# One encoder layer with a mixture of experts: the block arena closes behind the router, and expert weights are loaded four rows of a partition at a time

## The chip, the core and the metric

The kernel runs on one core of a Trainium2 chip. The core has five engines with instruction streams of their own: PE (matrix products), DVE and ACT (elementwise work), POOL (GpSimd) and SP, which in this kernel only issues DMAs and reads registers. Sixteen DMA engines move data between the chip's HBM and the core's SBUF, a memory of 128 partitions. The metric is the device time of one execution in microseconds (us); less is better. Of the kernel before three runs were timed: median 1249.86 us, from 1247.67 to 1251.27.

## What is computed

One layer for 256 tokens of width 1024, all in float32. Cut to what matters here:

```python
mod = silu(c) @ w_ada + b_ada                      # six vectors: shift, scale, gate for each half
h = x * (1 + scale1) + shift1
q_a, k_a, v_a, c_q, c_kv, k_rope, g_a, g_b = split(h @ w_in)
y_a = chunked_relpos_attention(q_a, k_a, v_a);  y_b = mla_attention(c_q, c_kv, k_rope)
merged = sigmoid(g_a) * (y_a @ w_branch_a) + sigmoid(g_b) * (y_b @ w_branch_b)
x = layer_norm(ALPHA * x + gate1 * (merged @ w_out), ln1_g, ln1_b)
h = x * (1 + scale2) + shift2
logits = h @ w_router + b_router                   # top 4 of 32 experts, softmax over the 4
f = sum over the 4 experts of weight * ((up + 1) * g * sigmoid(1.702 * g)) @ w_down[e] + ...
    # g = min(h @ w_gate[e] + b_gate[e], 7), up = clip(h @ w_up[e] + b_up[e], -7, 7)
x = layer_norm(ALPHA * x + gate2 * f, ln2_g, ln2_b)
```

Each of the 32 experts has three matrices of 1024 x 1024 float32, 4 MB each: 384 MB of weights that are read once.

## The kernel before

SBUF holds an **arena** `ar` of twenty blocks of 128 x 2048 float32 (8 KB of a partition, 1 MB each). `al()` takes the block that has been free the longest, `fr()` gives blocks back; a new tile on a block waits until the old one's readers are done. All large things live in such blocks one after the other: the activations, weights of the dense part in pieces, and later the expert weights. Small things that live long are in the pool `keep`, those of the middle phase in `p3` on the right side, those of the experts in `mp`.

The order of the instructions on each engine isn't that of the code: a scheduler places them by its own estimate of when each can run. So an edit in one place can move instructions elsewhere.

The program has three stretches.

- *Projections and attention* (to about 190 us). Products that need full float32 precision are made from a high and a low part of each operand: `split` (L150 to L153) casts the high part on ACT and subtracts it, L153, on DVE or POOL (each takes half of a block), and `mm3` multiplies high by high, high by low and low by high (L279 to L281). Meanwhile `w_ada` streams in and DVE sums it up (L640).
- *The middle* (about 190 to 293 us). The modulation vectors are finished (L687 to L752): POOL copies rows to all partitions with `partition_broadcast` (L739, L740, L745). `load_branch` brings `w_branch_a` and `w_branch_b` in four pieces (L765), splits each (DVE the half of branch a, POOL that of branch b), and PE makes `ba` and `bb` from them; `load_wo` does the same for `w_out` (L808) and PE makes `o`. Then come the first norm, the router and the gathering of tokens (`route`, `gather_first`, `weigh`).
- *The experts* (from 293 us). The tokens of an expert are gathered with a 0/1 matrix. First comes the group `s`, the experts 30 and 31; the other 30, sorted by load, fall into 13 groups of two or three, `e0` to `e12`, whose numbers SP reads from `order_i` at run time (L1285, 30 register loads). For each group and each of the three kinds (gate, up, down) `load_group` issues the weights on SP and 8 k-steps of matmuls use them (L1063: `sg`, `su`, `sd`, `e0g` and so on).

In `load_group` a partition's eight rows of 1024 floats are brought in four loads of two rows, 1 MB each:

```python
for kq in range(4):
    for j in range(n):
        v, r = al()
        v = v.rearrange("p (k n) -> p k n", k=2)
        if not (fine and kq == 3):
            SP.dma_start(v, aps[j][:, 2 * kq:2 * kq + 2, :])
```

and `mm` frees a block after every second k-step. For the last kind of the last group (`fine`) the last two rows come in two halves of the columns. Ahead of the middle's branch loads `hold(4)` (L756) takes four blocks out of the arena, which are given back behind the router (`freed.update(held)`). SP can issue expert weights into these four long before the experts begin. `take_late` takes two blocks for the experts' activations, `load_norm` two for the final norm. The hooks of the group `s` sort the experts: `sort_a` (counts and ranks, L1147 to L1157), `sort_b` (`order_i`, L1161, L1162), `sort_c` (`tokp`, L1172).

## Time and profile before

| | |
|---|---|
| median of 3 runs | 1249.86 us (1247.67 to 1251.27) |
| the profiled execution | 1245.99 us, span 1244.3 us |
| PE busy | 1103.0 us, 89% of the span |
| DVE, ACT, POOL busy | 362.8, 172.5, 123.0 us (29%, 14%, 10%) |
| read from HBM | 459.09 MB, 370 GB/s over the span |
| chain that ended last | DMA 48%, PE 36%, DVE 8%, issue 3% |

The span is the time between the first and the last instruction that the profiler recorded; the execution's own time is 1.7 us more. A busy share is an average over stretches that are limited by different things. The profile's idle times name the engine or the DMA that released an instruction; "issue" means that nothing was recorded that it waited for. DMA shares are shares of all 16 engines.

### The profile page before, as it was taken

How to read it: one execution, taken by the hardware profiler on the slowest of the kernel's cores; microseconds unless marked ns; L12 is line 12 of the kernel's file. 1: busy time of each engine (PE TensorE's matmuls, PEld its weight loads, DVE VectorE, ACT ScalarE, POOL GpSimd, SP SyncE). 2: the span in 40 equal slices, each digit the busy share in tenths (PEclk: the TensorE clock that was granted, in tenths of full speed). 3: DMA queues.
4: the chain of work that ended last, by engine and by line, in shares of the span. 5: the costliest groups of instructions: out<-in, count | busy, mean ns of one | idle time of the engine just before them, and what ended most of it. 6: DMA issues, size and time to landing. Idle time of an engine off the chain costs nothing.

```text
span 1244.3 us, 19465 instructions
## 1 busy us (share of the span) xinstructions
PE 1103.0 (89%) x8023; PEld 511.9 (41%) x8023; DVE 362.8 (29%) x704; ACT 172.5 (14%) x340; POOL 123.0 (10%) x140
## 2 busy tenths in 40 slices
PE   6889999797998989899989789889889999899995
PEld 4658885773242433434223223232233434343431
DVE  4868982684121121211012001011011211111113
ACT  3345552230000000000000000000000000000011
POOL 2211562433000000000000000000000000000001
PEclk8989998898999999899999999999999999999998
DMA  9958646398999999999999999999999999999992
GB/s 341 345 186 307 229 142 237 102 355 333 421 420 420 421 422 420 422 420 420 421 421 421 421 420 421 422 421 420 422 421 421 421 420 421 420 420 421 421 399 76
DMA packets 90333, 461.44 MB, mean 371 GB/s; under 512 B 8809, under 2 KB 33430, under 8 KB 39298
## 3 DMA queue, kind: packets, MB, share of 16 engines
q1 hardware_dynamic: 90242, 460.17, 91.6%
q8 instruction: 64, 1.05, 0.3%
q14 instruction: 27, 0.22, 0.0%
HBM read 459.09 MB, written 1.05 MB: 370 GB/s over the span
## 4 chain that ended last, share of the span: by engine, by line
DMA 48%; PE 36%; DVE 8%; issue 3%; SPq 2%; ACT 1%; POOL 1%; DVEq 0%; ACTq 0%; POOLq 0%
DMA blk<-in_w_down_dram 19%; DMA blk<-in_w_up_dram 14%; DMA blk<-in_w_gate_dram 13%; DVE blk L640 1%; PE e2d L1063 1%; PE e0d L1063 1%; PE sg L1063 1%; PE e12d L1063 1%; PE e3d L1063 1%; PE e1d L1063 1%; PE sd L1063 1%; PE e3u L1063 1%; PE e2u L1063 1%; PE e1u L1063 1%; PE e0u L1063 1%
## 5 line engine op out<-in xcount | busy, mean ns | idle before, releaser
L153 POOL TENSOR_TENSOR blk<-blk,blk 128x512 fp32r<-128x512 f32 (+2 forms) x44 | 84.8, 1948 | 148.8 <-ACT blk L152 80.5
L1298 POOL COPY sel<-sel 96x64 bf16<-96x64 bf16 (+2 forms) x30 | 5.9, 230 | 807.5 <-PE e5d L1132 90.4
L152 ACT CAST blk<-blk 128x512 fp32r<-128x512 f32 (+2 forms) x76 | 54.1, 767 | 41.5 <-DVE blk L798 16.6
L1092 ACT ACTIVATE blk<-blk 128x512 f32<-128x512 f32 x28 | 17.2, 630 | 234.0 <-DVE blk L1090 234.0
L153 DVE TENSOR_TENSOR blk<-blk,blk 128x512 fp32r<-128x512 f32 (+2 forms) x32 | 39.0, 1227 | 33.7 <-ACT blk L152 23.0
L640 DVE SCALAR_TENSOR_TENSOR blk<-blk,csil,blk 128x1024 f32<-128x1024 f32 x28 | 41.8, 1537 | 1.3 <-DMA blk<-in_w_ada_dram 1.2
L281 PE MATMUL g<-blk,blk 128*128 128x256 f32 x128 | 36.6, 291 | 2.0 <-POOL blk L153 2.0
L279 PE MATMUL g<-blk,blk 128*128 128x256 f32 x128 | 36.8, 288 | 0.0
L280 PE MATMUL g<-blk,blk 128*128 128x256 f32 x128 | 36.1, 282 | 0.0
L1063 PE MATMUL e7u<-blk,xgb 128*32 128x512 f32 x128 | 25.3, 599 | 4.5 <-DMA blk<-in_w_up_dram 4.5
L1063 PE MATMUL e5u<-blk,xgb 128*32 128x512 f32 x128 | 25.6, 599 | 4.0 <-DMA blk<-in_w_up_dram 4.0
L1063 PE MATMUL e6u<-blk,blk 128*32 128x512 f32 x128 | 25.3, 599 | 4.0 <-DMA blk<-in_w_up_dram 4.0
L1063 PE MATMUL e5d<-blk,xgb 128*32 128x512 f32 x128 | 23.2, 656 | 3.6 <-DMA blk<-in_w_down_dram 3.4
L281 PEld LDWEIGHTS g<-blk,blk 128*128 128x128 f32 x128 | 24.2, 191 | 4.3 <-POOL blk L153 2.9
L1063 PE MATMUL e7d<-blk,blk 128*32 128x512 f32 x128 | 22.7, 597 | 3.0 <-DMA blk<-in_w_down_dram 2.7
L279 PEld LDWEIGHTS g<-blk,blk 128*128 128x128 f32 x128 | 24.5, 191 | 0.9 <-issue 0.6
L1063 PE MATMUL e6d<-blk,xgb 128*32 128x512 f32 x128 | 22.4, 621 | 2.5 <-DMA blk<-in_w_down_dram 2.5
L1063 PE MATMUL e4d<-blk,blk 128*32 128x512 f32 x128 | 22.1, 613 | 2.8 <-DMA blk<-in_w_down_dram 2.8
L280 PEld LDWEIGHTS g<-blk,blk 128*128 128x128 f32 x128 | 24.5, 191 | 0.0
L1063 PE MATMUL e4u<-blk,xgb 128*32 128x512 f32 x128 | 20.6, 596 | 2.0 <-DMA blk<-in_w_up_dram 2.0
L1063 PE MATMUL e6g<-blk,blk 128*32 128x512 f32 x128 | 19.4, 596 | 1.8 <-DMA blk<-in_w_gate_dram 1.8
L1063 PE MATMUL e7g<-blk,xgb 128*32 128x512 f32 x128 | 19.4, 595 | 1.7 <-DMA blk<-in_w_gate_dram 1.7
(745 smaller groups left out, 1919.2 us busy)
## 6 DMA issues: line engine op xcount, KB each, us to landing
blk<-in_w_gate_dram SPq DMA_DIRECT2D x128, 1024.0 KB, 19.7
blk<-in_w_up_dram SPq DMA_DIRECT2D x128, 1024.0 KB, 19.8
blk<-in_w_down_dram SPq DMA_DIRECT2D x126, 1024.0 KB, 19.8
blk<-in_w_ada_dram SPq DMA_DIRECT2D x24, 1024.0 KB, 9.6
blk<-in_w_in_dram SPq DMA_DIRECT2D x12, 1024.0 KB, 5.4
blk<-in_w_in_dram SPq DMA_DIRECT2D x8, 592.0 KB, 11.4
blk<-in_w_out_dram SPq DMA_DIRECT2D x4, 1024.0 KB, 6.0
blk<-in_w_branch_a_dram SPq DMA_DIRECT2D x4, 512.0 KB, 3.7
```

Of the source, the lines that this page charges most:

```text
L152: A.copy(hi, src)
L153: (V if eng == "V" else G).tensor_sub(lo, src, hi.bitcast(F32))
L279: T.matmul(o, sh, mh, start=first, stop=False)
L280: T.matmul(o, sh, ml, start=False, stop=False)
L281: T.matmul(o, sl, mh, start=False, stop=last)
L640: eng.scalar_tensor_tensor(acc_v[:, sl], v[:, q * D:(q + 1) * D], csil[:, k:k + 1], acc_v[:, sl], op0=ALU.mult, op1=ALU.add)
L1063: T.matmul(pss[hf][c0:c0 + m, :], stat[:, k, c0:c0 + m], ch[par][k // 2][:, k % 2, hf * 512:(hf + 1) * 512], start=(k == 0), stop=(fine an ...
L1092: A.activation(s, g[:, sl], AF.Sigmoid, scale=SW_ALPHA)
L1298: G.tensor_copy(sel[:, lo:lo + n], sel96[:, r:r + 1].to_broadcast([96, n]))
```

## The change

- The arena is no longer open to the end. Behind the router it is closed, and a new pool `ax` takes its bytes with ten blocks `wt0` to `wt9` of 128 x 4096 (16 KB of a partition, 2 MB). They are taken in the order in which pairs of the old blocks came free, by `al2` and `fr2`.
- `load_group` loads four rows of a partition in one DMA of 2 MB, in place of two of 1 MB; a block is freed after every fourth k-step. In the last kind the last four rows come as one load of two rows and two halves of the last two. `take_late` and `load_norm` take one big block each, and the loop for overfull experts (not run with these inputs) loads in the same way.
- `hold(4)` becomes `hold(0)`: no blocks are kept out of the arena, and so no expert weights can be issued before its blocks come free at the end of the middle.
- `keep` moves to the right side, below `p3`, and `mp` takes the bytes of `p3` on the right.

```diff
--- before.py
+++ after.py
@@ -117,7 +117,8 @@
 
     nb = [2]
     psum_phase("psum1")
-    ar = ctx.enter_context(tc.tile_pool(name="ar", bufs=1, side="left", reuse_waits="tile"))
+    ar_cm = tc.tile_pool(name="ar", bufs=1, side="left", reuse_waits="tile")
+    ar = ar_cm.__enter__()
     freed = {i: i - NB for i in range(NB)}
     clock = [0]
 
@@ -128,13 +129,15 @@
         clock[0] += 1
         return ar.tile([P, BLK], dt, tag=f"blk{i}", bufs=1, name=f"blk{i}_{clock[0]}"), i
 
-    held = {}
+    held = []
 
     def hold(n):
 
         for _ in range(n):
-            i = min(freed, key=freed.get)
-            held[i] = freed.pop(i)
+            i = min((i for i in range(0, NB, 2) if i in freed and i + 1 in freed),
+                    key=lambda i: max(freed[i], freed[i + 1]))
+            del freed[i], freed[i + 1]
+            held.append(i // 2)
 
     def fr(*blocks):
         for i in blocks:
@@ -670,9 +673,9 @@
     fr(hTh_r, hTl_r, qk_r, bva[0][1], bva[1][1])
 
     p2_cm.__exit__(None, None, None)
+    keep = ctx.enter_context(tc.tile_pool(name="keep", bufs=1, side="right", reuse_waits="tile"))
     p3_cm = tc.tile_pool(name="p3", bufs=1, side="right", reuse_waits="tile")
     p3 = p3_cm.__enter__()
-    keep = ctx.enter_context(tc.tile_pool(name="keep", bufs=1, side="left"))
 
 
     psum_phase("psum3")
@@ -753,7 +756,7 @@
     g2n, b2p = scale2, shift2
 
 
-    hold(4)
+    hold(0)
     for b in range(2):
         A.activation(gT[b], gT[b], AF.Sigmoid)
     WB = []
@@ -981,10 +984,30 @@
     fr(mgh_r, mgl_r, rt_r, ms_r, rwa_r, rwb_r)
 
     p3_cm.__exit__(None, None, None)
-
-
-    freed.update(held)
-    mp = ctx.enter_context(tc.tile_pool(name="mp", bufs=1, side="left", reuse_waits="tile"))
+    order_freed = sorted(range(NB // 2), key=lambda d: (d not in held, max(freed.get(2 * d, 0), freed.get(2 * d + 1, 0))))
+    ar_cm.__exit__(None, None, None)
+
+
+    ax = ctx.enter_context(tc.tile_pool(name="ax", bufs=1, side="left", reuse_waits="tile"))
+    mp = ctx.enter_context(tc.tile_pool(name="mp", bufs=1, side="right", reuse_waits="tile"))
+    slots_ax = [ax.tile([P, 2 * BLK], F32, tag=f"wt{d}", bufs=1, name=f"wt{d}_0") for d in range(NB // 2)]
+    fresh = set(range(NB // 2))
+    freed = {d: n for n, d in enumerate(order_freed)}
+    clock[0] = NB
+
+    def al2():
+        d = min(freed, key=freed.get)
+        del freed[d]
+        clock[0] += 1
+        if d in fresh:
+            fresh.discard(d)
+            return slots_ax[d], d
+        return ax.tile([P, 2 * BLK], F32, tag=f"wt{d}", bufs=1, name=f"wt{d}_{clock[0]}"), d
+
+    def fr2(d):
+        clock[0] += 1
+        assert d not in freed
+        freed[d] = clock[0]
 
 
     late = {}
@@ -993,7 +1016,8 @@
 
     def take_late():
         if not late:
-            a, b = al()[0], al()[0]
+            ab = al2()[0]
+            a, b = ab[:, 0:BLK], ab[:, BLK:2 * BLK]
             late["g"] = a[:, 0:D]
             late["s"] = [a[:, D + i * 512:D + (i + 1) * 512] for i in range(2)]
             late["y"] = [b[:, i * 512:(i + 1) * 512] for i in range(2)]
@@ -1006,19 +1030,21 @@
     def load_group(aps, fine=False):
         n = len(aps)
         ch, regs = [[] for _ in range(n)], [[] for _ in range(n)]
-        for kq in range(4):
+        for kh in range(2):
             for j in range(n):
-                v, r = al()
-                v = v.rearrange("p (k n) -> p k n", k=2)
-                if not (fine and kq == 3):
-                    SP.dma_start(v, aps[j][:, 2 * kq:2 * kq + 2, :])
+                v, r = al2()
+                v = v.rearrange("p (k n) -> p k n", k=4)
+                if not (fine and kh == 1):
+                    SP.dma_start(v, aps[j][:, 4 * kh:4 * kh + 4, :])
+                else:
+                    SP.dma_start(v[:, 0:2, :], aps[j][:, 4:6, :])
                 ch[j].append(v)
                 regs[j].append(r)
         if fine:
             for hf in range(2):
                 sl = slice(hf * 512, (hf + 1) * 512)
                 for j in range(n):
-                    SP.dma_start(ch[j][3][:, :, sl], aps[j][:, 6:8, sl])
+                    SP.dma_start(ch[j][1][:, 2:4, sl], aps[j][:, 6:8, sl])
         return ch, regs
 
     ptb = [pt0, mp.tile([P, 2, P], F32, name="pt1")]
@@ -1061,7 +1087,7 @@
             def step(k, hf):
                 for c0, m, par in segs:
                     T.matmul(pss[hf][c0:c0 + m, :], stat[:, k, c0:c0 + m],
-                             ch[par][k // 2][:, k % 2, hf * 512:(hf + 1) * 512],
+                             ch[par][k // 4][:, k % 4, hf * 512:(hf + 1) * 512],
                              start=(k == 0), stop=(fine and k == 7), skip_group_check=True)
 
             for k in range(8):
@@ -1073,9 +1099,9 @@
                 elif not (fine and k == 7):
                     for hf in range(2):
                         step(k, hf)
-                if k % 2 == 1:
+                if k % 4 == 3:
                     for rg in regs:
-                        fr(rg[k // 2])
+                        fr2(rg[k // 4])
                 if (name, k) in hooks:
                     hooks[(name, k)]()
             if not fine:
@@ -1233,7 +1259,8 @@
     fin = []
 
     def load_norm():
-        fin_v, o_v = al()[0], al()[0]
+        fo = al2()[0]
+        fin_v, o_v = fo[:, 0:BLK], fo[:, BLK:2 * BLK]
         lnr = o_v[0:1, :].rearrange("p (a n) -> p a n", a=2)
         SP.dma_start(lnr[:, 0, :], ln2_g)
         SP.dma_start(lnr[:, 1, :], ln2_b)
@@ -1322,10 +1349,10 @@
         def get_w(kind):
             ch, regs = [], []
             src = dyn_rows(weights[kind], e_dyn)
-            for kq in range(4):
-                v, r = al()
-                v = v.rearrange("p (k n) -> p k n", k=2)
-                SP.dma_start(v, src[:, 2 * kq:2 * kq + 2, :])
+            for kh in range(2):
+                v, r = al2()
+                v = v.rearrange("p (k n) -> p k n", k=4)
+                SP.dma_start(v, src[:, 4 * kh:4 * kh + 4, :])
                 ch.append(v)
                 regs.append(r)
             return [ch], [regs]
```

Up to the router the lines of the changed kernel are those of before plus 3, from there on plus 26.

The scheduler sets the instructions anew. The first place is POOL, where the modulation vectors and the branch weights are prepared. `L739 ISA` without operands is a change of the library that POOL runs, the rows with operands on L739, L740 and L745 are broadcasts, `blk_186` is the low part of a piece of `w_in`. Before:

```order
L153 TENSOR_TENSOR blk_186_1887<-blk_164_1607,blk_185_1886 128x512 x3
L739 ISA
L739 ISA blk_200_1966<-blk_199_1965 128x1024
L699 MEMSET ones_p 128x128
L740 ISA b1r<-blk_199_1965 128x1024
L947 MEMSET zero_bf 128x128
```

With the change (lines plus 3):

```order
L742 ISA
L742 ISA blk_200_1966<-blk_199_1965 128x1024
L156 ISA
L156 TENSOR_TENSOR blk_186_1887<-blk_164_1607,blk_185_1886 128x512 x3
L702 MEMSET ones_p 128x128
L743 ISA
L743 ISA b1r<-blk_199_1965 128x1024
L950 MEMSET zero_bf 128x128
```

The split of `blk_186` has moved behind the first broadcast, and the two broadcasts stand apart: three changes of library where there was one. Further on, where `blk_206`, `blk_210`, `blk_218` and `blk_224` are the low parts of the four pieces of branch weights, before:

```order
L153 ISA
L153 TENSOR_TENSOR blk_206_2048<-blk_204_2044,blk_205_2047 128x1024
L745 ISA
L745 ISA blk_199_1965<-blk_201_1967 128x512 x4
L745 ISA blk_200_1966<-blk_201_1967 128x512 x2
L745 ISA gate_2024<-blk_201_1967 128x512 x2
L153 ISA
L153 TENSOR_TENSOR blk_210_2057<-blk_208_2053,blk_209_2056 128x1024
L153 TENSOR_TENSOR blk_218_2118<-blk_216_2114,blk_217_2117 128x1024
L153 TENSOR_TENSOR blk_224_2182<-blk_222_2178,blk_223_2181 128x1024
```

With the change:

```order
L156 ISA
L156 TENSOR_TENSOR blk_218_2118<-blk_216_2114,blk_217_2117 128x1024
L156 TENSOR_TENSOR blk_206_2048<-blk_204_2044,blk_205_2047 128x1024
L748 ISA
L748 ISA blk_199_1965<-blk_201_1967 128x512 x4
L156 ISA
L156 TENSOR_TENSOR blk_210_2057<-blk_208_2053,blk_209_2056 128x1024
L748 ISA
L748 ISA blk_200_1966<-blk_201_1967 128x512 x2
L748 ISA gate_2024<-blk_201_1967 128x512 x2
L156 ISA
L156 TENSOR_TENSOR blk_224_2182<-blk_222_2178,blk_223_2181 128x1024
```

In these rows the last piece is split behind five changes of library, where it was behind three; with the rows above them POOL has eight ahead of the splits of `w_out`, where it had four.

The second place is SP in the first expert groups, where `order_i` is the sorted list of experts. Before, the 30 register loads are spread between weight loads, here behind the first five of them:

```order
L1285 TENSOR_LOAD order_i
L1285 ISA x2
L1014 DMA blk_305_2908<-in_w_down_dram 128x2048
L1014 DMA blk_306_2910<-in_w_down_dram 128x2048
L1285 TENSOR_LOAD order_i
L1285 ISA x2
```

With the change all 30 stand in one run, between the ninth weight load and the tenth; its end reads:

```order
L1312 TENSOR_LOAD order_i
L1312 ISA x2
L1038 DMA wt_39_2885<-in_w_down_dram 128x4096
L1038 DMA wt_40_2887<-in_w_down_dram 128x4096
L1038 DMA wt_41_2889<-in_w_down_dram 128x4096
L1038 ISA
L1038 DMA wt_46_3032<-in_w_gate_dram 128x4096
```

There are no register loads behind it, and none of the refills is ahead of it.

The third place is PE at the start of the experts. Before, `order` and `tokT` stand behind half of `sg`:

```order
L1063 MATMUL sg_2689<-blk_267_2677,xgb_2643 32x512 x2
L1063 MATMUL sg_2689<-blk_268_2679,xgb_2643 32x512 x2
L1063 MATMUL sg_2690<-blk_267_2677,xgb_2643 32x512 x2
L1063 MATMUL sg_2690<-blk_268_2679,xgb_2643 32x512 x2
L1161 MATMUL order<-perm,ecol 1x32
L1166 MATMUL tokT<-ident,posm 32x128 x2
L1166 MATMUL tokT<-ident,wtok 32x128 x2
L1063 MATMUL sg_2689<-blk_269_2681,xgb_2643 32x512 x2
L1063 MATMUL sg_2689<-blk_270_2683,xgb_2643 32x512 x2
```

With the change they, and `tokp` and `sel`, stand ahead of its first matmul:

```order
L1078 MATMUL sws<-wtok,pt_2323 32x1 x7
L1187 MATMUL order<-perm,ecol 1x32
L1192 MATMUL tokT<-ident,posm 32x128 x2
L1192 MATMUL tokT<-ident,wtok 32x128 x2
L1198 MATMUL tokp<-perm,tokT 128x32 x4
L1201 MATMUL sel_2785<-perm,rep_117 96x32
L1089 MATMUL sg_2691<-wt_0_2651,xgb_2657 32x512 x2
L1089 MATMUL sg_2692<-wt_0_2651,xgb_2657 32x512 x2
```

So the list of experts no longer waits for half of `sg`.

## Rows read from the trace of the kernel before

**Rows 1.** The page, its part 2: busy tenths in 40 slices.
```profile
DMA  9958646398999999999999999999999999999992
```

**Rows 2.** Windows: us, busy us of each engine, PE clock, DMA share, GB/s.
```profile
600.00:800.00 200.00, 173.77 (x1031) 54.95 (x1024) 22.19 (x40) 8.27 (x14) 1.07 (x6) 0.98 1.01 421
```

**Rows 3.** Timeline of POOL, 190 to 240 us: start, us, engine, line, idle before.
```profile
193.71 1.30 POOL L739 PARTITION_BROADCAST blk<-blk  x1 [8.01 <-issue]
...
207.35 2.37 POOL L153 TENSOR_TENSOR blk<-blk,blk 128x1024 fp32r<-128x1024 f32 x1 [10.87 <-issue]
215.72 4.12 POOL L745 PARTITION_BROADCAST blk<-blk  x6 [6.00 <-issue]
...
229.84 8.62 POOL L153 TENSOR_TENSOR blk<-blk,blk 128x1024 fp32r<-128x1024 f32 x3 [7.74 <-ACT blk L152]
```

**Rows 4.** Instructions of L739 and L153 on POOL's queue: durations in ns, first and last start.
```profile
L739 POOLq MODIFY_POOL_CONFIG  x2: 8/8/8, 185.7 to 185.7; - x2
...
L153 POOLq MODIFY_POOL_CONFIG  x4: 127/128/128, 196.4 to 222.0; - x4
```

**Rows 5.** Windows of POOL's four idle times, and of 296.5 to 299.8 us.
```profile
185.70:193.70 8.00, 7.25 (x53) 5.85 (x51) 4.72 (x9) 0.00 (x0) 0.00 (x0) 1.00 0.82 260
196.40:207.35 10.95, 10.95 (x24) 1.48 (x22) 2.45 (x2) 5.88 (x7) 0.08 (x2) 1.00 0.81 312
209.90:215.70 5.80, 5.80 (x29) 5.80 (x29) 0.00 (x0) 0.00 (x0) 0.00 (x0) 0.50 0.24 82
222.00:229.80 7.80, 1.31 (x11) 1.10 (x10) 4.87 (x10) 4.92 (x6) 0.10 (x1) 0.92 0.33 115
296.50:299.80 3.30, 3.30 (x33) 1.21 (x29) 0.00 (x0) 0.00 (x0) 0.00 (x0) 0.96 0.13 20
```

**Rows 6.** Timeline of ACT: the casts ahead of POOL's split at 229.84.
```profile
222.43 1.98 ACT L152 CAST blk<-blk 128x1024 fp32r<-128x1024 f32 x2
```

**Rows 7.** Timeline of PE in the branch products.
```profile
232.23 0.58 PE L281 MATMUL bb<-blk,blk 128*128 128x256 f32 x1 [8.92 <-POOL blk L153]
...
245.41 0.28 PE L281 MATMUL bb<-blk,blk 128*128 128x256 f32 x1
```

**Rows 8.** Timelines of DVE and PE at the start of the experts.
```profile
294.55 0.23 DVE L1157 TENSOR_SCALAR perm<-iota_e,rank 32x32 f32<-32x32 f32 x1
...
293.40 8.72 PE L1063 MATMUL sg<-blk,xgb 128*32 128x512 f32 x63
302.06 0.21 PE L1161 MATMUL order<-perm,ecol 32*1 32x32 f32 x2
...
302.74 7.07 PE L1063 MATMUL sg<-blk,xgb 128*32 128x512 f32 x64
```

**Rows 9.** Timeline of SP's queue: the issues of weight loads.
```profile
253.52 5.96 SPq L1014 DMA_DIRECT2D blk<-in_w_gate_dram  x4
...
291.38 0.33 SPq L1014 DMA_DIRECT2D blk<-in_w_up_dram  x1
298.71 8.76 SPq L1014 DMA_DIRECT2D blk<-in_w_down_dram  x6
311.51 14.38 SPq L1014 DMA_DIRECT2D blk<-in_w_gate_dram  x8
```

**Rows 10.** Instructions of L1285 on SP's queue: durations in ns, first and last start.
```profile
L1285 SPq TENSOR_LOAD <-order_i x30: 260/267/472, 303.0 to 326.5; - x30
L1285 SPq FUSED_REGOPS  x30: 147/147/178, 303.5 to 326.8; - x30
```

**Rows 11.** DMA view of 250 to 254 us (2 KB rows) and of 700 to 800 us.
```profile
DMA packets 762, 1.53 MB, mean 382 GB/s; under 512 B 16, under 2 KB 16, under 8 KB 762
...
DMA packets 5772, 42.07 MB, mean 421 GB/s; under 512 B 641, under 2 KB 641, under 8 KB 641
```

**Rows 12.** Chain of waits near the end: start, us, what.
```profile
1199.82 3.63 PE e12u L1063 x24
```

**Rows 13.** Timeline of POOL near the end.
```profile
1210.47 1.30 POOL L1241 PARTITION_BROADCAST blk<-blk  x1 [105.76 <-DMA blk<-in_ln_g_dram]
```

## Prediction

> **What bounds the kernel now.** The row of the page on the DMA engines comes first: of the 40 slices the first ten are mixed, and from the eleventh to the last but one they are full [rows 1]. The windows view of 600 to 800 us says what that is: 421 GB/s at a share of 1.01 while PE is busy 174 of 200 us [rows 2]. From about 300 us to the landing of the last expert weights the time is bytes over rate (the last `up` load lands at 1199.8 [rows 12], and the 8.4 MB of `down` behind it take 19.9 us at 421 GB/s, so 1219.7), and the rest of PE hides behind it. Ahead of that stretch the kernel is a chain through PE, DVE, ACT and POOL with DMA only partly used; whatever delays the moment at which the weight stream gets going is paid in full, since nothing behind it has room. So the change has four places where it can cost or gain: POOL's work ahead of the branch products, the moment at which the stream starts for good, the rate of the stream, and the tail.
>
> **POOL, 183 to 260 us.** The scheduler orders POOL anew, as the order rows under the change show. An `ISA` row without operands is a change of the library that POOL runs (recorded as a pair of MODIFY_POOL_CONFIG, so four records on L153 are two changes) [rows 4]. Before has four of them in a row between broadcasts and splits; the changed order has eight. What one costs is read from POOL's idle time ahead of its next instruction: 8.01, 10.87, 6.00 and 7.74 us, together 32.6 [rows 3]. Two of these hold more or less than the price. The 7.74 is put down to an ACT cast, and that cast ended at 222.43 + 1.98 = 224.4, so 5.4 us of it came after the data were there [rows 6]. And the 8.01 and 10.87 stand in stretches with the DMA engines 0.82 and 0.81 busy, while 6.00 and 7.74 stand where they were 0.24 and 0.33 busy [rows 5]. The busy stretches are those in which 4 MB of gate weights run into the four held blocks, which the change no longer has. So the changed kernel's eight fall into quieter time; the bounds are 5.4 and 8.15 (the mean of the four), and I take 6.5, nearer to the quiet rows. Eight make 52.0, against 32.6: the last split of the branch weights, which ended at 229.84 + 8.62 = 238.5, moves to 257.9. It is not needed at once: PE starts on the branch products at 232.23, when the split before it is there, and reaches the first product with that last POOL half (the third matmul of the last `bb`) at 245.41 [rows 7]. So 6.9 us of the shift are slack and **12.4 us** of delay reach the output projection, the norm and the router behind it, where PE, DVE and ACT hand over to each other without a pause that could take it up. With 5.4 it is 3.9, with 8.15 it is 25.7. The three splits of `blk_186`, now behind the first change, cost nothing more: the same POOL time, counted in the shift.
>
> The Trainium skill, "GPSIMD Engine Reference", section 2.1 (Instruction dispatch), says that the first call into a freshly loaded library waits about 6 us, measured 5.95, with no instruction of its own in a profile. The 6.00 us row agrees [rows 3]; the 10.87 doesn't, unless the load was held up. By the page's figure the delay would be 8 x 5.95 - 32.6 - 6.9 = 8.1 us and the whole sum 4.3 us less.
>
> **When the stream starts for good.** Before, SP has issued 18 loads of 1 MB when all its blocks are full (four into held blocks, fourteen from 253.52 to 291.38 [rows 9]); they have landed by 296.5, the DMA engines idle until 299.8 (share 0.13 [rows 5]), and the first refill goes out at 298.71, when two k-steps of `sg` have freed blocks [rows 9]. After, the stock is the same 18 MB (nine loads of 2 MB; one of the ten blocks is kept for activations). The four early gate loads are thus a wash: they come later, but the stream waits for the first free block in both kernels. What moves is that block's refill. Blocks come free after k = 3 instead of k = 1: `sg`'s 128 matmuls take 8.72 + 7.07 us, 3.9 per two k-steps, so at least +3.9. But a longer wait takes its place. In the changed order all 30 register loads of the expert ids (L1285, on SP) stand in one run between the ninth load and the first refill, and the `order` matmul that they wait for is ahead of `sg`. That run starts earlier: `perm` is ready at 294.55 + 0.23 = 294.8, the matmul and its cast take 0.4 (they started at 302.06, the first register load at 303.0), so it begins about 295.7 [rows 8, 10]. One is 0.27 + 0.15 = 0.42 us on the queue [rows 10], and the six that stand between the last `down` (ends 307.47) and the first `gate` (311.51) took 4.04, 0.67 each with what they waited for. In between, 0.55: 16.5 us, so SP is free at 312.2 plus the delay from POOL. That is **13.5 us** behind 298.71 (9.6 with 0.42, 17.1 with 0.67). The nine loads don't last so long: they start about when the first gate load behind `w_out` did, 253.52 plus some 14 us, and 18.9 MB at 421 GB/s last 45 us, to about 313, while the refill lands in the queue at 325. The `s` group's products of `down` need what is loaded then; six MB take 15 us and PE gets there some 17 us after the refill begins, so PE doesn't fall behind.
>
> **The rate of the stream.** A partition's row of a load grows from 8 to 16 KB. Rows of 2 KB ran at 382 GB/s, of 8 KB at 421 [rows 11]: over 16 engines 85.8 and 311.3 ns a row, so 37.6 ns per KB and 10.6 fixed. A 16 KB row would take 612 ns, which is 428 GB/s; 921 us (298.7 to 1219.7) shrink by 1.65%, **-15 us**. No row of 16 KB weights is in the trace. The bounds are nothing (each row is moved as two of 8 KB) and -31 us (the fixed part is gone altogether, 10.6 of 311.3).
>
> **The tail.** When the last `up` load lands, 3.63 us of its products are left, 24 matmuls of two k-steps [rows 12]; with a load of four k-steps it is twice that, **+3.6 us** (bounds 0 and 5: some of it may hide in the landing of `down`). The last `down` keeps its two fine pieces.
>
> At nothing: `keep` and `mp` change sides (`mp` takes `p3`'s bytes, so its first writes wait for `p3`'s last readers, the router's own instructions, which end before); the refills' issue itself (half as many DMAs); the two late library changes, since the broadcast behind the first of them comes after 105.8 us of waiting for a DMA [rows 13].
>
> **Sum.** 12.4 + 13.5 - 15 + 3.6 = +14.5 us. The profiled execution took 1245.99 us (span 1244.3), 3.9 below the median of 1249.86, so it becomes 1260.5 and the median 1264.4. About 0.3% (3.7 us) is what a measurement of this kernel can tell from no change.
>
> **Rivals.**
> - *The larger rows bring nothing.* For it: the share is 1.01 already, and rows of 8 KB carry only 3% of fixed time. Against: the rise from 2 to 8 KB. Sum without the gain: +29.5, 1279. Chance 0.14.
> - *A library change costs what it cost on average*, 8.15, since the branch loads and `w_ada` load the DMA engines in its place: +27.8, 1277.7. Against it the 6.00 row. Chance 0.12.
> - *POOL's changes are hidden* (the load of the library runs while POOL's next instruction waits for data anyway, as with the late ones [rows 13]): the first term goes, +2.1, 1252, no change. It decides if idle times in the new order are waits on casts. Against it: three of the four idle times are put to nothing that the profile shows. Chance 0.07.
> - *Not slower: the stream itself runs at the rate without the fixed part*, from 300 to 1220 us. Each GB/s is worth some 2.2 us, and from 434 GB/s on (packets of 16 KB in under 604 ns) the sum is 1.9 us or less; at 435.7 it is -1.5 with my other terms, 1248.4, and -10 with the cheapest library change. Against it: it asks for twice the gain that the step from 2 to 8 KB gives. Chance 0.09, half of it faster.
>
> Beside the last one: the Trainium skill, "DMA: Bandwidth & Descriptors", section "Where 436 GB/s comes from", puts the ceiling of 16 engines at 435.2 GB/s, and 358 for what one core draws from HBM. The 421 of the trace refutes the second for this kernel; by the first the gain ends at 30 us.
>
> **How the numbers follow.** The forecast itself (+14.5, slower) has 0.55; cheap library changes with the rest as forecast (+6) are part of it. Slower is 0.55 + 0.14 + 0.12 = 0.81, and 0.02 more for delays not thought of; faster is half of the last rival, and 0.03 for a stream that never idles because its stock lasts past the register loads; same is what remains. The range reaches from just under the hidden changes (1250.5) to just over the two slow rivals (1280).
>
> **What would show it.** In the profile after: eight pairs of MODIFY_POOL_CONFIG between 180 and 260 us with idle gaps of 5.4 to 8 us behind each, and the last split of branch weights near 258; PE waiting for POOL a second time within `ba`/`bb`; the router's `sxg` matmuls some 12 us later; an idle DMA stretch of about 10 us that ends with SP's first refill near 325, behind a run of 30 register loads; the stream at 428 GB/s in packets of 16 KB; about 7 us of `e12u` behind its last landing. The forecast is wrong if the gaps behind the changes are short or lie within waits for casts, if the stock covers the register loads, or if the stream stays at 421 or goes beyond 434.

## The result and the profile after

The changed kernel took 1262.99 us, the median of four runs (1261.46 to 1269.3), against 1249.28 for the kernel before, measured again: a ratio of 1.0119, interval 1.008 to 1.0157. It is slower by 1.2%, 13.7 us; the forecast was +14.5. The profiled execution took 1261.46 us (span 1259.8); its span is 15.5 us longer than that of before. Of all the runs in this document one execution, the fourth of experiment 7, took 5263 us; it is left out there.

The page's part 2, the lines on DMA, answers to [rows 1]:

```profile
DMA  9958742259799999999999999999999999999991
GB/s 340 338 184 319 249 141 95 100 237 397 300 429 424 428 426 427 428 426 427 427 428 428 427 428 426 430 427 428 427 428 428 426 427 427 426 427 428 427 373 45
```

The seventh slice (189 to 220 us) is emptier than before, where the early gate loads ran (2 tenths for 6), and so is the ninth (252 to 283 us, 5 for 9); the eleventh (315 to 346 us) has a hole (300 GB/s), and from the twelfth the stream moves 424 to 430 GB/s. Three moments cut the span into the stretches that the prediction spoke of: `perm`, with which the list of experts is sorted, SP's first refill, and the landing of the last `up` load. Two more lie ahead of them: the **mark**, at which POOL ends a wait of 10.41 us for PE and begins the last splits of pieces of `w_in`, and the end of `blk_181`'s splits among these.

| stretch | before | after | difference | forecast |
|---|---|---|---|---|
| start to the mark | 161.10 | 161.60 | +0.5 | 0 |
| to the end of `blk_181`'s splits | 18.45 | 15.30 | -3.15 | 0 |
| to `perm` ready | 115.2 | 127.9 | +12.7 | +12.4 |
| to the first refill | 3.9 | 18.2 | +14.3 | +13.5 |
| to the last `up` landing | 901.1 | 887.6 | -13.5 | -15 |
| to the end | 44.5 | 49.1 | +4.6 | +3.6 |
| span | 1244.3 | 1259.8 | +15.5 | +14.5 |

The second row belongs to the change. Up to the mark POOL and PE run the same instructions in the same order in both kernels. DVE from 155 us on and ACT from 160 us on don't, and in the kernel before POOL waits for a cast of ACT in the middle of the splits that follow:

```profile
161.10 10.14 POOL L153 TENSOR_TENSOR blk<-blk,blk 128x512 fp32r<-128x512 f32 x6 [10.41 <-PE g L281]
174.32 1.31 POOL L153 TENSOR_TENSOR blk<-blk,blk 128x512 fp32r<-128x512 f32 x1 [3.07 <-ACT blk L152]
175.78 9.92 POOL L153 TENSOR_TENSOR blk<-blk,blk 128x512 fp32r<-128x512 f32 x5 [0.16 <-ACT blk L152]
```

(The last three of the x5 are those of `blk_186`.) From the mark to `perm` it is 133.7 us before and 143.2 after: the middle costs 9.5 us, not 12.7.

POOL's timeline of 160 to 285 us (start, us, engine, line, [idle before <- releaser]) answers to [rows 3]:

```profile
161.60 15.30 POOL L156 TENSOR_TENSOR blk<-blk,blk 128x512 fp32r<-128x512 f32 x9 [10.41 <-PE g L284]
182.47 1.30 POOL L742 PARTITION_BROADCAST blk<-blk  x1 [5.56 <-PE pT L613]
190.54 3.73 POOL L156 TENSOR_TENSOR blk<-blk,blk 128x512 fp32r<-128x512 f32 x3 [6.77 <-DVE blk L626]
...
200.42 1.30 POOL L743 PARTITION_BROADCAST b1r<-blk  x1 [6.01 <-ACT blk L652]
...
209.15 4.64 POOL L156 TENSOR_TENSOR blk<-blk,blk 128x1024 fp32r<-128x1024 f32 x2 [7.27 <-ACT blk L155]
219.74 3.07 POOL L748 PARTITION_BROADCAST blk<-blk  x4 [5.95 <-issue]
231.54 2.33 POOL L156 TENSOR_TENSOR blk<-blk,blk 128x1024 fp32r<-128x1024 f32 x1 [8.73 <-issue]
239.75 1.48 POOL L748 PARTITION_BROADCAST blk<-blk  x2 [5.88 <-issue]
...
250.48 8.46 POOL L156 TENSOR_TENSOR blk<-blk,blk 128x1024 fp32r<-128x1024 f32 x3 [6.98 <-PE ba L284]
```

From 182.47 on, eight idle times, one at each change of POOL's library, from subtractions to broadcasts or back, together 53.15 us; 8 x 6.5 = 52.0 was the forecast. They fall into two kinds: ahead of a broadcast 5.56 to 6.01, ahead of a subtraction 6.77 to 8.73. The names of releasers (`pT`, `ba`) say little here, since the gap follows the change, not the named work. Of the x3 at 250.48 only the first is a split of branch weights, the last one, and it ends at 252.82; the other two belong to `w_out`. Four of those idle times, as windows:

```profile
194.60:200.40 5.80, 5.80 (x39) 4.35 (x38) 1.22 (x1) 3.14 (x4) 0.00 (x0) 0.99 0.05 10
201.80:209.10 7.30, 7.30 (x17) 1.02 (x16) 1.23 (x1) 2.58 (x3) 0.08 (x1) 1.00 0.52 171
214.00:219.70 5.70, 5.70 (x47) 5.31 (x46) 2.13 (x6) 2.48 (x3) 0.00 (x0) 1.00 0.00 0
222.70:231.50 8.80, 2.80 (x24) 2.60 (x22) 0.00 (x0) 0.00 (x0) 0.10 (x1) 0.85 0.33 119
```

The second last column is the share of the DMA engines. In the last of these PE, too, is busy for only 2.80 of 8.80 us: it waits for the POOL half that follows, as before [rows 7]. New are two more kinds of waits on PE in the branch products, a second one for POOL (for that last branch split) and short ones for DVE:

```profile
233.92 0.58 PE L284 MATMUL bb<-blk,blk 128*128 128x256 f32 x1 [8.42 <-POOL blk L156]
243.49 0.39 PE L282 MATMUL bb<-blk,blk 128*128 128x256 f32 x1 [1.51 <-DVE blk L800]
...
252.87 0.58 PE L284 MATMUL bb<-blk,blk 128*128 128x256 f32 x1 [2.28 <-POOL blk L156]
```

At the start of the experts, the timelines of DVE, of PE and of SP's queue with its first refill, which answer to [rows 8, 9]:

```profile
304.58 0.23 DVE L1183 TENSOR_SCALAR perm<-iota_e,rank 32x32 f32<-32x32 f32 x1
...
304.86 0.26 PE L1187 MATMUL order<-perm,ecol 32*1 32x32 f32 x2 [1.26 <-DVE perm L1183]
...
309.02 16.53 PE L1089 MATMUL sg<-wt,xgb 128*32 128x512 f32 x128
...
323.04 2.84 SPq L1038 DMA_DIRECT2D wt<-in_w_down_dram  x3
```

And the register loads on that queue (durations in ns, first and last start) [rows 10]:

```profile
L1312 SPq TENSOR_LOAD <-order_i x30: 260/267/468, 305.4 to 322.4; - x30
```

They fill SP's queue from 305.4 to 322.9, and the first refill follows at 323.04. The windows there, and of the stream [rows 2]:

```profile
300.00:310.00 10.00, 5.06 (x44) 3.55 (x48) 6.52 (x28) 0.55 (x2) 2.00 (x2) 0.50 1.00 427
310.00:320.00 10.00, 10.00 (x80) 2.83 (x76) 0.12 (x1) 0.00 (x0) 0.76 (x4) 0.79 0.38 161
320.00:330.00 10.00, 10.00 (x94) 3.21 (x90) 2.58 (x4) 1.23 (x2) 0.00 (x0) 1.00 0.62 236
...
600.00:800.00 200.00, 160.05 (x1091) 54.70 (x1089) 23.89 (x46) 9.36 (x16) 1.13 (x6) 0.95 1.01 427
```

Two stretches of 10 us at shares of 0.38 and 0.62 are 10 us without transfers, in one hole. In the stream the rate is 427, and the DMA view of 700 to 800 us shows half as many packets as [rows 11]:

```profile
DMA packets 2941, 42.79 MB, mean 428 GB/s; under 512 B 329, under 2 KB 329, under 8 KB 329
```

The end of the chain of waits [rows 12]: the last `up` load, then 7.06 us of products of four k-steps.

```profile
1177.83 32.80 DMA wt<-in_w_up_dram
...
1210.68 7.06 PE e12u L1089 x56
```

### The profile page after: what moved, and what is told of

It reads as the page before. It is cut to its first block, busy times and chain, and to the rows that moved or that the text cites. A ratio compares the mean times of both kernels' runs of the same rounds, so it can differ in the third digit from the quotient of the medians.

```text
span 1259.8 us, 18738 instructions
## 1 busy us (share of the span) xinstructions
PE 1083.7 (86%) x8023; PEld 510.5 (41%) x8023; DVE 362.2 (29%) x704; ACT 172.3 (14%) x340; POOL 121.3 (10%) x140
## 4 chain that ended last, share of the span: by engine, by line
PE 42%; DMA 33%; DVE 5%; issue 3%; ACT 1%; POOL 1%; SPq 0%; DVEq 0%; POOLq 0%; ACTq 0%
DMA wt<-in_w_up_dram 22%; DMA wt<-in_w_down_dram 11%; PE sg L1089 1%; PE e10d L1089 1%; PE e9d L1089 1%; PE e2d L1089 1%; PE e0d L1089 1%; PE e10u L1089 1%; PE e12d L1089 1%; PE e3d L1089 1%; PE e8d L1089 1%; PE e11d L1089 1%; PE e3g L1089 1%; PE e1d L1089 1%; PE sd L1089 1%
## 5 line engine op out<-in xcount | busy, mean ns | idle before, releaser
L155 ACT CAST blk<-blk 128x512 fp32r<-128x512 f32 (+2 forms) x76 | 54.1, 769 | 42.1 <-DVE blk L801 13.7
L1089 PE MATMUL e6u<-wt,wt 128*32 128x512 f32 x128 | 23.2, 708 | 7.3 <-DMA wt<-in_w_up_dram 7.3
L1089 PE MATMUL e4u<-wt,xgb 128*32 128x512 f32 x128 | 23.3, 712 | 7.1 <-DMA wt<-in_w_up_dram 7.0
L1089 PE MATMUL e5u<-wt,xgb 128*32 128x512 f32 x128 | 20.5, 654 | 8.7 <-DMA wt<-in_w_up_dram 8.7
L1089 PE MATMUL e7u<-wt,xgb 128*32 128x512 f32 x128 | 19.7, 654 | 8.0 <-DMA wt<-in_w_up_dram 8.0
L1089 PE MATMUL e6d<-wt,xgb 128*32 128x512 f32 x128 | 21.1, 706 | 4.2 <-DMA wt<-in_w_down_dram 3.9
L1089 PE MATMUL e7d<-wt,wt 128*32 128x512 f32 x128 | 19.4, 608 | 4.1 <-DMA wt<-in_w_down_dram 3.9
L1089 PE MATMUL e5d<-wt,xgb 128*32 128x512 f32 x128 | 19.3, 608 | 4.2 <-DMA wt<-in_w_down_dram 4.0
L1089 PE MATMUL e4d<-wt,wt 128*32 128x512 f32 x128 | 19.2, 607 | 4.3 <-DMA wt<-in_w_down_dram 4.1
L1089 PE MATMUL e5g<-wt,xgb 128*32 128x512 f32 x128 | 19.0, 641 | 3.0 <-DMA wt<-in_w_gate_dram 3.0
L1089 PE MATMUL e6g<-wt,wt 128*32 128x512 f32 x128 | 17.7, 594 | 4.5 <-DMA wt<-in_w_gate_dram 4.5
```

What stands on the lines that cost most here:

```text
L155: A.copy(hi, src)
L1089: T.matmul(pss[hf][c0:c0 + m, :], stat[:, k, c0:c0 + m], ch[par][k // 4][:, k % 4, hf * 512:(hf + 1) * 512], start=(k == 0), stop=(fine an ...
```

## Experiments

The theory: the four terms are independent, and each belongs to one piece of the change (POOL's eight changes to `hold(0)`, the late refill to the run of register loads, the rate to the row of 16 KB, the tail to the block of four k-steps). Its rivals: the four early gate loads are themselves worth time to the stream; the refill waits for PE and not for SP; the rate comes from fewer and larger blocks and not from the row. All ratios are to the kernel before, run on the same chip (medians 1250.0 to 1250.6), and "before" and "after" name the two kernels.

**One caution for all that follows.** POOL and PE reach the mark by the same instructions in the same order everywhere, and yet it came between 161.1 and 168.5 us in these profiles. So stretches are compared from the mark on, and times by their medians. The end of `blk_181`'s splits, from which the expectations below count, will not do: it follows 15.3 us behind the mark in after and the experiments with its order (1 to 4, 6, 7), and 18.4 to 18.6 us in before and those with blocks held (5, 8, 9, 10).

### 1. `hold(0)` alone, in the kernel before

```diff
-    hold(4)
+    hold(0)
```

> The kernel before with hold(0) in place of hold(4) and nothing else. Theory (the change's loss has two parts, POOL's eight library changes and the register loads in one run; hold(0) brings the first alone): POOL has the eight changes, perm is ready some 10 us later than 294.8 as in the changed kernel (304.8), the register loads stay spread between 1 MB loads, the first refill comes about 5 us after the start of sg, and the end is 10 us later than before, about 1259 us. Rival A (the four early gate loads matter by themselves, since 4.2 MB at 421 GB/s are 10 us of stream): another 5 to 10 us on top, 1264 to 1269 us. Rival B (POOL's order costs nothing, the later middle of the changed kernel comes of the new pools): within 2 us of before.

Measured: 1267.94 us, 1.0138 [1.0104, 1.0172]. POOL has the same eight changes as after. To `perm` it takes 150.8 us from the mark (before 133.7, after 143.2), and the first refill still follows 3.8 us behind `perm`, the register loads standing between the weight loads as before; the stream runs at 421. So the POOL term belongs to `hold(0)` and the refill term does not. The extra 7.6 us over after come from SP's queue, whose timeline reads:

```profile
231.16 16.12 SPq L808 DMA_DIRECT2D blk<-in_w_out_dram  x2
264.20 0.35 SPq L1014 DMA_DIRECT2D blk<-in_w_gate_dram  x1
264.65 0.38 SPq L808 DMA_DIRECT2D blk<-in_w_out_dram  x1
267.54 0.35 SPq L1014 DMA_DIRECT2D blk<-in_w_gate_dram  x1
267.99 0.38 SPq L808 DMA_DIRECT2D blk<-in_w_out_dram  x1
```

A gate load that waits for a free block stands ahead of the third and the fourth `w_out` load, which the output projection needs. That was not expected, and experiment 6 takes it away. The time lies in rival A's range, but not for its reason (experiments 6 and 9).

### 2. After, with the branch splits behind the last broadcast: four changes

```diff
-            G.partition_broadcast(dst[:, hf * 512:(hf + 1) * 512], rows32[...])
+            spread = G.partition_broadcast(dst[:, hf * 512:(hf + 1) * 512], rows32[...])
...
-        for br in range(2):
-            split(v[:, br, :, :], hi[:, br, :, :], lo[:, br, :, :], "VG"[br])
+        with tc.issue_after(spread.ins):
+            for br in range(2):
+                split(v[:, br, :, :], hi[:, br, :, :], lo[:, br, :, :], "VG"[br])
```

> The changed kernel with POOL's subtractions of the branch weights queued behind the last broadcast, so that POOL has four library changes in place of eight, none of them between branch pieces; hold(0) and the loads stay. Theory (the library changes are the 10 us of the middle): the last split of branch weights ends about 20 us earlier than 258.9, perm is ready at about 295 in place of 304.8, and the time falls by 8 to 10 us to about 1254 us. Rival (the middle is late since the branch weights are loaded into blocks that come free later without held blocks, or since the early loads are gone): perm stays at 303 to 305 and the time within 2 us of 1263.

Measured: 1255.45 us, 1.0042 [1.0027, 1.0058], so 0.8% less than after by the two ratios. To `perm` 135.1 us, 8.1 less than after; the refill again 18.2 us behind `perm`. Four changes fewer return 8.1 of the POOL term's 9.5, and the refill term stands unmoved beside it. POOL also idles 5.75 us between two broadcasts here without a change of library: its queue waits for the rows until 213.04 us. So not every such idle time is a change. (The 258.9 of the expectation is the end of a `w_out` split; the last branch split ends 15.9 us earlier here than after, counted from the mark.)

### 3. After, with the register loads behind the weight loads sent so far

```diff
-        ids = [nc.sync.value_load(order_i[0:1, r:r + 1], ...) for r, _ in group]
+        with tc.issue_after(sent[-1].ins):
+            ids = [nc.sync.value_load(order_i[0:1, r:r + 1], ...) for r, _ in group]
```

(`sent` collects the weight loads of `load_group`.)

> The changed kernel with the register loads of each group queued behind the last weight load of the group before, so that none stands ahead of the first refill. Theory (the run of 30 register loads holds the first refill, 17.5 us from order_i to 322.9): the first refill goes out when sg's k = 3 frees its blocks, near 317.5, the idle stretch of the DMA engines shrinks by 5 to 6 us, and so does the time, to about 1257 us. Rival (the coarser release holds it, the register loads only fill a wait): the refill stays near 323 and the time within 2 us of 1263.

Measured: 1260.06 us, 1.0079 [1.0042, 1.0116]; its interval overlaps with that of after, so the stretch decides. `perm` is ready at 309.42; PE and SP then:

```profile
313.63 15.62 PE L1091 MATMUL sg<-wt,xgb 128*32 128x512 f32 x128
...
322.39 1.86 SPq L1040 DMA_DIRECT2D wt<-in_w_down_dram  x2
```

The refill comes 13.0 us behind `perm`, not 18.2: only 5.3 of the 14.3 go with the register loads, and the time is 3 us above the theory's. What then holds it is PE: 8.8 us from the start of `sg` to the block that k = 3 frees (5.3 for k = 1 before, from 293.40 to 298.71 [rows 8, 9]), and `sg` itself starts 4.2 us behind `perm`, with `order`, `tokT`, `tokp` and `sel` ahead of it, where before it started 1.4 us ahead of it. The rival had a part in it: two waits lay one over the other, and the prediction had put the shorter at 3.9 us in place of 9.0. Experiment 4 agrees: there only 12 register loads stand ahead of the first refill, and it comes 13.1 us behind `perm`, 8.9 behind the start of `sg`.

### 4. After, with each block filled by two loads of two rows (8 KB)

```diff
-                    SP.dma_start(v, aps[j][:, 4 * kh:4 * kh + 4, :])
+                    for q in range(2):
+                        SP.dma_start(v[:, 2 * q:2 * q + 2, :], aps[j][:, 4 * kh + 2 * q:4 * kh + 2 * q + 2, :])
```

> The changed kernel with each 2 MB block filled by two loads of two rows (8 KB of a partition) in place of one of four. Theory (the stream's gain comes of the longer rows): 421 GB/s in packets of 8 KB between 400 and 1200 us, last weights 13.5 us later, less some 3.5 us in the tail since the products of a block's first two rows need not wait for its last two: about 1273 us. Rival (the gain comes of the bigger blocks and their coarser release, or of fewer DMAs to issue and to wait for): still 427 GB/s, 1259 to 1263 us.

Measured: 1276.61 us, 1.0213 [1.0183, 1.0243]. From the first refill to the last `up` landing 902.3 us, as before (901.1), against 887.6 after. Its DMA view of 700 to 800 us and the end of its chain:

```profile
DMA packets 5771, 42.08 MB, mean 421 GB/s; under 512 B 638, under 2 KB 638, under 8 KB 638
```

```profile
1206.22 19.44 DMA wt<-in_w_up_dram
1225.70 7.06 PE e12u L1090 x56
```

So the rate doesn't belong to the blocks: with the same blocks and queue, 8 KB rows bring back 421 GB/s. The loads are twice as many here, too, so the run alone doesn't part the row from the load; the packets do. Between 700 and 800 us the 16 engines are full in both kernels (share 1.01). A packet of 8 KB takes 313 ns here (median), one of 16 KB 614 after, 12 less than two of 8 KB. The small packets (under 512 B), which halve with the number of loads, take 9 ns each: 638 of them here against 329 are 3 us of the 1600 that the engines have, 0.2 of the 1.7%. The rest goes with the row. The miss is the tail: 7.06 us of products still stand behind the last landing, though that landing brings two k-steps only. The products of a block began only when all of the block was there. The tail belongs to the block, not to the load.

### 5. After, with `hold(2)`: two pairs held back, as many blocks as before held

```diff
-    hold(0)
+    hold(2)
```

> The changed kernel with hold(2) in place of hold(0): two pairs of blocks are kept out of the arena, POOL has four library changes again, expert weights still start behind w_out's loads. Theory (library changes are the loss of the middle, 12.7 us from the end of blk_181's splits to perm): that stretch returns to about 115 us (before 115.2, after 127.9) and the time falls by 11 to 13 us, to 1250 to 1252 us. Rival (half of it is other work that the new order delays, as the grouped order kept 4.6 of the 12.7): 1255 to 1257 us.

Measured: 1254.57 us, 1.0036 [1.0018, 1.0054]. The time is 2.6 us above the theory's 1250 to 1252. POOL's timeline:

```profile
196.01 1.30 POOL L742 PARTITION_BROADCAST blk<-blk  x1 [5.67 <-issue]
...
214.12 2.37 POOL L156 TENSOR_TENSOR blk<-blk,blk 128x1024 fp32r<-128x1024 f32 x1 [7.19 <-issue]
222.36 1.48 POOL L748 PARTITION_BROADCAST blk<-blk  x2 [5.88 <-PE ba L284]
...
233.34 8.63 POOL L156 TENSOR_TENSOR blk<-blk,blk 128x1024 fp32r<-128x1024 f32 x3 [7.24 <-issue]
```

Four changes, as before, but 26 us in place of 32.6: without 4 MB of gate loads beside them the first two cost 5.67 and 7.19 where before showed 8.01 and 10.87 [rows 3]. To `perm` 133.1 us from the mark (before 133.7), from there to the refill 17.6. So the middle is back, and against before the later refill (+13.7), the faster stream (-13.7) and the tail (+3.8) remain: with the -0.6 they make +3.2, and the medians differ by 4.1. The theory had left out that the other terms don't quite cancel. The eight changes come from the number of held blocks, and not from the pairs or from the wider loads.

### 6. `hold(0)` in the kernel before, expert loads behind all `w_out` loads

```diff
-    hold(4)
+    hold(0)
...
-                    SP.dma_start(v, aps[j][:, 2 * kq:2 * kq + 2, :])
+                    with tc.issue_after(wo_sent[-1].ins):
+                        SP.dma_start(v, aps[j][:, 2 * kq:2 * kq + 2, :])
```

> The kernel before with hold(0), as in the first experiment, but with every expert weight load queued on SP behind the four loads of w_out. Theory (of that run's 17 us some 10 are the library changes and some 7 a new wait: three gate loads that wait for a free block stand ahead of w_out's third and fourth load): w_out's splits end about 7 us earlier against the branch splits, and the time is 1259 to 1262 us. Rival (the lost early gate loads cost the 7 us by themselves): 1266 to 1269 us.

Measured: 1260.09 us, 1.0084 [1.0055, 1.0114], so +9.6 us. To `perm` 143.8 us, 7.1 less than experiment 1 and 0.5 from after. The detour of the `w_out` loads was experiment 1's surplus; the rest, +10.1 against before, is what the order with eight changes in place of four costs here, and the time shows it as well.

### 7. Experiment 2, with one more trip to the broadcasts and back

A broadcast into a spare tile, which nobody reads, between the first and the last POOL halves of the branch weights:

```diff
+        if jp == 3:
+            with tc.issue_after(halves[-1].ins):
+                spread2 = G.partition_broadcast(spare, rows32[0:1, 0, :])
```

> The grouped order of the second experiment (1255.5 us) with one more broadcast, into a spare tile that nobody reads, between the POOL halves of the third and the fourth piece of branch weights: two more library changes. Theory (6.0 us into the broadcast library, 7.1 back, and the broadcast 0.8, less the slack of some 7 us that the last piece has): the last split ends 14 us later, perm 5 to 8 us later against the start of POOL's stretch, and the time is 1261 to 1263 us. Rival A (changes are hidden in waits for casts): within 2 us of 1255.5. Rival B (there is no slack): 1269 us.

Measured: 1266.44 us (median of three), 1.0132 [1.0101, 1.0162], 11 us more than experiment 2; the profiles' spans differ by 7.0. POOL's timeline:

```profile
246.97 0.80 POOL L780 PARTITION_BROADCAST spare<-blk  x1 [7.38 <-DVE blk L158]
255.93 10.80 POOL L158 TENSOR_TENSOR blk<-blk,blk 128x1024 fp32r<-128x1024 f32 x4 [8.15 <-issue]
```

The last branch split ends 16.3 us later than in experiment 2 (7.38 + 0.80 + 8.15 = 16.3), counted from the mark, PE now waits 9.0 us for it, and `perm` comes 7.3 later. So a little less than half of the trip is paid, and the rest is hidden behind PE's products. The price of a change is shown directly; the median's 11 us is more than the stretch explains, and the rest stays open.

### 8. After, with the costs found so far taken out

`hold(2)`, the splits of experiment 2, the register loads of experiment 3, the matmuls that sort behind the steps of `sg`, and the last four rows of the last `up` weights in two loads:

```diff
-    hold(0)
+    hold(2)
...
-                    hooks[(name, k)]()
+                    with tc.issue_after(done[0].ins):
+                        hooks[(name, k)]()
...
+        if half:
+            for q in range(2):
+                for j in range(n):
+                    SP.dma_start(ch[j][1][:, 2 * q:2 * q + 2, :], aps[j][:, 4 + 2 * q:6 + 2 * q, :])
```

(`done` holds the last matmul of the expert step, so the hook's sorting matmuls stand behind it.)

> The changed kernel with two pairs held, the branch splits on POOL behind all broadcasts (two library changes ahead of them in place of eight), the register loads of a group behind the last weight load of the group before, the expert sort's matmuls behind the k-steps of sg that the code puts them behind, and the last up weights with their last four rows in two loads. Theory (the terms of the change can be undone one by one while the 13.5 us of the longer rows stay): middle -10 to -12, refill -5.3, earlier sg -4, tail -2 to -3.5 against 1263: 1239 to 1243 us, below both kernels. Rival (the gain of the rows is given back in another wait once the stream starts earlier, for instance PE behind the stream): 1247 to 1252 us.

Measured: 1243.07 us, 0.9937 [0.9917, 0.9956]: faster than both kernels. POOL has two changes (5.53 and 7.42 us idle), to `perm` it takes 131.2 us from the mark (after 143.2), and the refill follows 5.1 us behind `perm` (after 18.2): 25.2 us less than after. But the profiles' spans differ by only 16.4. The mark came 2.2 us later in this execution, and from the refill to the end it takes 943.4 us instead of 936.7. The chain shows the latter:

```profile
1136.31 7.06 PE e11u L1099 x56
1148.31 14.64 PE e11d L1099 x128
1171.85 13.78 PE e12g L1099 x128
1186.17 13.89 PE e12u L1099 x128
```

After its landing at 1136.31 no weight load stands in it any more: PE bounds the last 107 us. The stream, started 23 us earlier, ends ahead of PE, and what it gains beyond that is lost: the time is the theory's upper end, and the wait that the rival named is there.

### 9. The kernel before, its four held blocks kept, but the gate loads behind `w_out`

The diff is that of experiment 6 with `hold(4)` kept.

> The kernel before, its four blocks held as they are, but with every expert weight load queued on SP behind the four loads of w_out: the early gate loads go, everything else stays, four library changes too. Theory (the early loads are worth nothing to the stream, since it stops for its first free block in both cases, and they slow the library loads): POOL's four idle times fall from 8.0, 10.9, 6.0 and 7.7 us to about 5.7, 7.2, 5.7 and 7.2; perm no later against blk_181's splits than 115 us; the DMA engines no longer idle ahead of the first refill; the time within 3 us of before. Rival A (the early loads carry part of the stream): 8 to 10 us slower, 1258 to 1260 us. Rival B (the long idle times were waits for data): the gaps stay at 8 and 11 us.

Measured: 1257.08 us, 1.0044 [1.002, 1.0069]. The expectation took POOL's order as that of before; it was not: the scheduler gave six changes, and `perm` comes 136.4 us behind the mark (before 133.7). So the time doesn't tell what early loads are worth. Two views do: POOL's idle times without gate loads beside them, and the DMA engines around the first refill.

```profile
204.80 2.33 POOL L153 TENSOR_TENSOR blk<-blk,blk 128x1024 fp32r<-128x1024 f32 x1 [7.58 <-ACT blk L152]
212.90 2.80 POOL L745 PARTITION_BROADCAST blk<-blk  x4 [5.77 <-issue]
223.57 2.39 POOL L153 TENSOR_TENSOR blk<-blk,blk 128x1024 fp32r<-128x1024 f32 x1 [7.88 <-issue]
```

```profile
300.00:305.00 5.00, 5.00 (x37) 1.67 (x33) 0.40 (x2) 0.00 (x0) 0.00 (x0) 0.68 1.01 421
```

The engines stay full through the refill at 304.76, and from there to the last `up` landing it takes 903.0 us, as before. Late gate loads fill the pause that before has at 296.5 to 299.8 [rows 5] and cost the stream nothing that shows: the rival that early loads are worth time has nothing for it.

### 10. Experiment 8 without the last `up` load in two

> The mended kernel (1243.1 us) without the split of the last up weights. Theory (PE, no longer the landing of the last up load, sets the last 93 us there, so the split does nothing): within 2 us of 1243. Rival (the two smaller loads save the products behind the last landing): 3 to 4 us slower, 1246 to 1247 us.

Measured: 1245.91 us, 0.9966 [0.9943, 0.9989]. That lies between theory and rival, and the interval overlaps with that of experiment 8, so whether the two loads are worth 0 or 3 us stays open; here, too, PE bounds the end: from 1110 us on no weight load stands in the chain.

## Why the prediction was right

The forecast was 1264.4 us and slower; it came to 1262.99. The terms one by one:

- **POOL, +12.4; measured +9.5** from the mark to `perm`. The mean price of 6.5 met 6.64 (53.15 / 8), but for half of the reason. The prediction split the four known gaps by how busy the DMA engines were; that holds for the two dear ones (experiment 5). What it missed is the direction: a change to the broadcasts is the cheaper one, a change back the dearer, and four of each average to about what was taken. The idle times grew by 20.5 us (19.4 said), but the prediction took them for the whole shift: the splits up to `blk_181`'s end came 3.15 us sooner, and POOL's own work behind them ran 3.5 us shorter. So the last branch split ended 13.9 us later against the mark, not 19.4. The slack was the 6.9 that it gave (245.41 against 238.47), and PE reached that split's product 7.0 us late. (Its remark that PE starts on the branch products at 232.23 is a misreading: PE goes on there after a wait of 8.92 us [rows 7].) Behind it 2.6 us were lost that it had at nothing: 1.5 in the last products of `bb`, where the granted clock was 0.62 (252.9 to 257.2 us, mostly the lower level, 1.2 GHz) after PE's wait of 2.28 us and 1.00 before (245.4 to 248.2, behind products without a wait), and 1.0 further on that was not traced.
- **The price by the page.** The rows ahead of a broadcast show 5.56 to 6.01 us, those ahead of a subtraction 6.77 to 8.73. The Trainium skill, "GPSIMD Engine Reference", section 2.1 (Instruction dispatch), gives 5.95 for the first call into a freshly loaded library. With the first kind this agrees, with the second it doesn't; an estimate of eight times 5.95 is 5.6 us short of the 53.15.
- **The refill, +13.5; measured +14.3.** The run of register loads took 17.5 us from `order_i` to its end (16.5 said) and does decide when the refill goes out. But the sentence that blocks come free "at least +3.9" later was mis-sized: without the register loads the refill is 9.0 us later than before, 3.4 of it for k = 3 and 5.6 because the sorting matmuls now stand ahead of `sg` (experiment 3). The prediction saw that move and used it for the register loads only. The sum was right since the longer wait covers the shorter; what undoing either alone brings back would have been forecast wrong.
- **The rate, -15; measured -13.5.** 427 to 428 GB/s, as the two rows of [rows 11] gave by their straight line; a packet of 16 KB took 614 ns (612 said). Up to the last `up` landing the stretch is 901 us; 421 to 427 is 12.7 us less of it, 421 to 428 is 14.7, and 13.5 lies between. The size of the term was right to 1.5 us.
- **The tail, +3.6; measured +4.6.** The products behind the landing took 7.06 instead of 3.63, as said. Of the rest, six products of `e12c` behind them took 4.28 us instead of 2.58, at a granted clock of 0.69 (in part the lower level) instead of 1.00 (1220.7 to 1226.2 us; before, 1206.4 to 1210.2), though PE had idled 2.7 us shortly ahead of them in both; the end behind `e12d` was 0.5 us shorter.
- **The start, 0; measured +0.5** up to the mark: same work, other execution.

The mechanism was right in all four places. That the sum came so close, though, is partly luck: POOL's term was 2.9 us too high, and the refill, the stream and the tail together cost 3.3 us more than said. The lower bound of the POOL term, 3.9, is 3.7 by its own figures.

The rivals: rows that bring nothing are ruled out by 887.6 against 901.1 us and by the packets of experiment 4. A change at 8.15 is ruled out by the 6.64. Hidden changes are ruled out by experiments 2, 6 and 7, each of which moves `perm` by 7 to 10 us with the changes. A stream at the rate of 435 did not come: 427. The Trainium skill, "DMA: Bandwidth & Descriptors", section "Where 436 GB/s comes from", puts the ceiling at 435.2 GB/s, which the 427 doesn't contradict, and says that for transfers from HBM a limit of about 358 binds, which it does contradict. The early gate loads were a wash for the stream, as said.

## What to carry to other kernels

A change that was made for the transfers can be decided by the order that a scheduler builds around it: count what each engine's queue now has in front of the step that matters, above all switches between kinds of work and loads of registers ahead of DMA issues. Where two waits lie one over the other, price both: the sum needs only the longer, but the remedy needs both; here the register loads alone brought the refill 5.3 us nearer to `perm`, with the sorting matmuls behind `sg`'s steps as well it was 13.1 (experiment 8). And larger blocks for longer rows pay with what waits for a whole block, at the first refill and at the last landing.

## What the runs showed of the hardware

- POOL's change of library costs by direction: without gate loads beside them 5.5 to 6.2 us to the broadcasts (7.38 in the extra trip of experiment 7) and 6.8 to 7.7 back to the subtractions, at some places 7.9 to 9.0. DMA traffic alone does not explain the dear ones: the 7.88 of experiment 9 stands in a stretch without any. What does stays open.
- Beside 4 MB of gate loads the first two changes cost 8.01 and 10.87 us [rows 3], without them 5.67 and 7.19 (experiment 5) or 5.86 and 7.58 (experiment 9).
- Rows of 16 KB run at 427 to 428 GB/s, of 8 KB at 421, with the same blocks: 614 and 313 ns a packet.
- A register load of an expert's number on SP takes 0.58 us in a run of 30 (17.5 us), and no weight load behind it in the queue can be issued meanwhile.
- The same instructions of POOL and PE reached the same point up to 7 us apart in different executions (the mark, 161.1 to 168.5 us).
